# First projection of a hybrid attention layer: another order for VectorE, with two of its operations one K-tile further ahead

## The chip, the core and the metric

The kernel runs on one core of a Trainium2 chip. The core has a matrix engine (TensorE, PE in the profile; its weight loads are listed apart as PEld), VectorE (DVE), ScalarE (ACT), GpSimd (POOL), and SyncE (SP), which here issues all transfers. Each engine works through its own list of instructions in order and waits at semaphores for the others. The metric is the time of one execution on the device in microseconds (us); lower is better.

## The reference

One decoder layer for 512 rows of 1024 values, in float32. A vector `c` gives a shift, a scale and a gate for each of the 1024 columns; the normalised input is scaled and shifted, and one large matrix `w_in` gives all queries, keys, values and gates of two groups of heads.

```python
mod = jax.nn.silu(c) @ w_ada + b_ada
shift, scale, gate = jnp.split(mod, 3, axis=-1)
h = rms_norm(x, norm_gain) * (1 + scale[:, None, :]) + shift[:, None, :]
proj = h @ w_in
...
o_a = banded_gqa(qa, ka, heads(v_a, A_KV), SWA_WINDOW, rel_bias[:, :A_HEADS], sinks)
...
o_cmp, o_sel = nsa_cmp_sel(qb, k_cmp, v_cmp, k_sel, heads(vs, B_KV), bias_b)
o_win = banded_gqa(qb, k_win, heads(vw, B_KV), NSA_WINDOW, bias_b, None)
...
return x + gate[:, None, :] * out
```

## The kernel before

**Splitting numbers.** Products are made with operands of reduced precision, each split in a high part and a low part, and summed as high times high, high times low, low times high. For weights the high part is a copy on ScalarE (line 269 in the first projection, line 175 later), and the low part a subtraction on VectorE (lines 272 and 176). For the input `h` the high part `hh` and a full copy `hf` are made on ScalarE (line 283), and the low part `hl` = `hf` - `hh` on VectorE (line 286).

**First projection.** It makes the 768 columns of queries, keys and values of head group A, for all 512 rows at once, in six banks of accumulators. The 1024 inner values are worked through in eight K-tiles of 128, numbered 0 to 7. For each, `first_proj(k, n)` issues three passes of eight matmuls: pass 0 is `hh` with the weights' high part, pass 1 `hh` with the weights' low part, pass 2 `hl` with the weights' high part (lines 293 and 294). A tile needs, ahead of these passes:

- its weights (`load_wst`, one transfer, a ring of four), `weights_high(k)` on ScalarE and `weights_low(k)` on VectorE. The tiles `swh` and `swl` are asked for with three buffers each;
- its input, transposed, times the rows' norm: `scaled(k, ...)` on VectorE (line 277), in place in `xTp`;
- its modulation, two columns of `AB`. For tiles 0 and 1 TensorE computes them (`mod_pe`, `mod_col`), and `mod_ab` puts them in place (lines 238 and 239). For tiles 2 to 7 VectorE does, in `mod_rows(k)`: two row sums over 1024 values of `w_ada` each (line 243, one for the shift and one for the scale, each followed by a short read-out of the accumulator) and a small product (line 249). The rows of `w_ada` come through a ring of four (`load_ada`);
- `h_high(k)` on ScalarE (line 283: `hh` in two halves, then `hf`), which reads the scaled input and `AB`, and `h_low(k)` on VectorE.

**What sets the order.** This part is written inside `in_order(tc)` (line 300), which ties each instruction to the one traced before it on the same engine. So what the code says there, from top to bottom, is each engine's order, SP's transfers included. In the loop of line 410, the loads for tile k + 4 come first, then passes 0 and 1 of tile k, then `new_tile(k + 1)`, then pass 2 of tile k. At k = 3 the table `rest` and the first weights of the later projections are queued on SP as well (`load_next`, line 156: two halves of `kv_cmp`, two of `kv_sel`, one of `kv_win_g`). At k = 7, `split_to("kv_cmp", 3, 0)` splits the weights `kv_cmp` in four pieces, taken in turn from the first and the second half (`raws[g, p % 2]`).

In `new_tile(k)` VectorE has the order: weights' low part of tile k, the two row sums and the product of tile k + 1, input's low part of tile k, scaling of tile k + 1. ScalarE has: `hh` and `hf` of tile k, weights' high part of tile k + 1.

**Behind it.** After the block come the squares of the queries and keys (line 444 and on), their norms (`prep_a`, with the row sums of line 568), the keys' scaling (line 549) and transposition on TensorE (line 554), and the attention of group A. Meanwhile TensorE is fed by further projections: `kv_cmp` (line 491, 48 matmuls), `kv_sel` and `kv_win_g` (line 481), and so on. There the order on each engine isn't written out by hand: a planner makes it from its own costs and due times, and assigns the memory, where tiles whose use doesn't overlap by its plan can share a place.

Of the kernel before, what the change touches and what calls it, by code (L numbers as in the profile page):

```python
# [34 lines left out]
PE_MOD = (0, 1)  # L35
# [47 lines left out]
def hybrid_layer_kernel(ctx, tc, A, out):  # L83
# [30 lines left out]
    cT, prm, ident = first[:, 0:8], first[:, 8:40], first[:, 40:168]  # L114
# [85 lines left out]
    ada, wst = {}, {}  # L200
# [14 lines left out]
    AB = con.tile([128, 8, 2], F32, name="AB")  # L215
# [19 lines left out]
    def mod_ab(k):  # L235

        pc = pcs.pop(k)
        DVE.tensor_tensor(AB[:, k, 1:2], pc[:, 0:1], prm[:, k:k + 1], op=OP.add)
        DVE.scalar_tensor_tensor(AB[:, k, 0:1], pc[:, 1:2], prm1[:, k:k + 1], prm[:, 24 + k:25 + k],
                                 op0=OP.add, op1=OP.mult)  # L240

    def row_sum(w, init, out):
        DVE.tensor_tensor_reduce(out=w, in0=w, in1=scb, scale=1.0, scalar=init, op0=OP.mult, op1=OP.add, accum_out=out)

    def mod_rows(k):

        row_sum(ada[k][:, 0], prm[:, k:k + 1], AB[:, k, 1:2])
        row_sum(ada[k][:, 1], prm1[:, k:k + 1], modt[:, k:k + 1])
        DVE.tensor_tensor(AB[:, k, 0:1], modt[:, k:k + 1], prm[:, 24 + k:25 + k], op=OP.mult)

# [15 lines left out]
    def weights_high(k):  # L266

        ws[k] = (stp.tile([128, 768], F32R, name="swh", bufs=3), stp.tile([128, 768], F32R, name="swl", bufs=3))
        ACT.activation(ws[k][0], wst[k], AF.Copy)

    def weights_low(k):
        DVE.tensor_tensor(ws[k][1], wst[k], ws[k][0].bitcast(F32), op=OP.subtract)

    def scaled(k, by, parts=(slice(0, S),)):
        y[k] = xT[k]
        for c in parts:
            DVE.tensor_tensor(y[k][:, c], xT[k][:, c], by[:, c], op=OP.mult)

    def h_high(k, parts=(slice(0, S),)):
        hf[k] = T2(F32, "hf")  # L280
        for t in (hh[k], hf[k]):
            for c in (parts if t is hh[k] else parts[:0] + (slice(0, S),)):
                ACT.activation(t[:, c], y[k][:, c], AF.Identity, bias=AB[:, k, 1:2], scale=AB[:, k, 0:1])

    def h_low(k):
        DVE.tensor_tensor(hl[k], hf[k], hh[k].bitcast(F32), op=OP.subtract)
# [13 lines left out]
    with in_order(tc) as begun:  # L300
# [85 lines left out]
        rb = stp.tile([128, S], F32, name="rb")  # L386
# [6 lines left out]
        scaled(1, rbp)  # L393
        h_low(0)
        weights_high(1)

        def new_tile(k):

            if k in PE_MOD:
                mod_ab(k)  # L400
            h_high(k, halves)
            weights_low(k)
            if k < 7:
                weights_high(k + 1)
                if k + 1 not in PE_MOD:
                    mod_rows(k + 1)
            h_low(k)
            if k < 7:
                scaled(k + 1, rb)
        for k in range(8):  # L410
            if k + NR < 8:
                load_ada(k + NR)
                load_wst(k + NR)
            if k == LW - 1:
                SP.dma_start(rest[:, 0:960], A["rest"])
                for _ in range(5):
                    load_next()
            first_proj(k, 0)
            if k + 1 in PE_MOD:
                for _ in mod_pe(k + 1):  # L420
                    pass
            first_proj(k, 1)
            if k + 1 in PE_MOD:
                mod_col(k + 1)
            if k < 7:
                new_tile(k + 1)
            first_proj(k, 2)
            if k == 7:
                split_to("kv_cmp", 3, 0)
# [683 lines left out]
```

## Time and profile before

| | |
|---|---|
| median of three runs | 315.12 us (314.93 to 315.32) |
| the profiled execution | 313.99 us |
| its span, first to last instruction | 312.0 us |
| granted TensorE clock | 1.00 throughout |
| first matmul of the first projection (line 293) | 15.01 us |
| first matmul behind it (line 491) | 53.28 us |

The page's chain of work that ended last, by engine and by line of the kernel:

```profile
PE 82%; DVE 11%; ACT 3%; DMA 2%; issue 1%; SPq 0%; DVEq 0%; ACTq 0%
PE pj L491 30%; PE s L885 8%; PE sq L293 8%; PE po L960 8%; PE pj L481 7%; PE pt L943 4%; PE pt L933 4%; PE skv L294 4%; PE s L610 3%; DMA xf<-in_xn 2%; DVE wl L176 2%; DVE qs L541 2%; PE po L966 1%; DVE pa L890 1%; DVE qn L529 1%
```

How to read the views. A row of the timeline has the start, the duration, the engine, the line of the kernel, the operation, the tiles written and read, the shapes and the count; in brackets stands idle time of the engine just ahead of it and what ended it. Consecutive starts are closer together than the durations say, since the end of one operation overlaps the start of the next; the distance from start to start is what an operation costs its engine. A row of the waits has who waited and for whom, the total in us, the times, and the longest. "Released by" is inferred by the profiler from semaphores. The first projection is some 12% of the span: lines 293 and 294 are 8% and 4% of the chain.

### The profile page before, as it was taken

To read this page: it belongs to the slowest core of one execution; us is meant where nothing else is said; L and a number is where in the kernel's file an instruction comes from. 1 tells how busy PE (TensorE), PEld (TensorE's weight loads), DVE (VectorE), ACT (ScalarE), POOL (GpSimd) and SP (SyncE) were. 2 spreads that over 40 slices of the span, in tenths; PEclk is the share of its full clock that TensorE was granted. 3 is DMA by queue.
4 is the path that set the end of the run, shared out by engine and by line. 5 is a ranking of instruction groups with operands and counts; after the bars stand their busy time and mean duration, and the time that the engine had idled before them with its cause. 6 is when DMAs were issued, how large, how long until landed. Compare 5 with 4: busy or idle time off the path is not lost.

```text
span 312.0 us, 5882 instructions
## 1 busy us (share of the span) xinstructions
PE 303.3 (97%) x2131; PEld 252.5 (81%) x2131; DVE 238.0 (76%) x665; ACT 196.5 (63%) x473; POOL 3.8 (1%) x21
## 2 busy tenths in 40 slices
PE   8899999999999999999999999999999999999995
PEld 4577788789988889989878688779788878788885
DVE  4769998999886467786999999986977887455221
ACT  5765468777967675967867657696667776413000
POOL 1000000000000000000000000000000000000000
PEclk9999999999999999999999999999999999999999
DMA  7998947890184734041341252304530150024401
GB/s 285 381 395 292 413 151 261 278 292 23 32 273 138 220 115 139 3 134 36 106 166 68 67 168 68 105 1 137 158 114 0 51 154 2 0 69 135 134 34 69
DMA packets 27420, 44.21 MB, mean 142 GB/s; under 512 B 1712, under 2 KB 19408, under 8 KB 27392
## 3 DMA queue, kind: packets, MB, share of 16 engines
q1 hardware_dynamic: 27392, 43.84, 41.7%
q8 instruction: 17, 0.28, 0.4%
q14 instruction: 11, 0.09, 0.1%
HBM read 41.70 MB, written 2.14 MB: 141 GB/s over the span
## 4 chain that ended last, share of the span: by engine, by line
PE 82%; DVE 11%; ACT 3%; DMA 2%; issue 1%; SPq 0%; DVEq 0%; ACTq 0%
PE pj L491 30%; PE s L885 8%; PE sq L293 8%; PE po L960 8%; PE pj L481 7%; PE pt L943 4%; PE pt L933 4%; PE skv L294 4%; PE s L610 3%; DMA xf<-in_xn 2%; DVE wl L176 2%; DVE qs L541 2%; PE po L966 1%; DVE pa L890 1%; DVE qn L529 1%
## 5 line engine op out<-in xcount | busy, mean ns | idle before, releaser
L176 DVE TENSOR_TENSOR wl<-raw,wh 128x512 fp32r<-128x512 f32 (+1 forms) x52 | 35.5, 692 | 17.1 <-PE pj L491 10.8
L175 ACT ACTIVATE wh<-raw 128x512 fp32r<-128x512 f32 (+1 forms) x52 | 31.4, 634 | 26.0 <-PE pj L491 25.0
L481 PE MATMUL pj<-wh,hh 128*128 128x256 f32 (+1 forms) x128 | 36.7, 287 | 0.0
L481 PE MATMUL pj<-wl,hh 128*128 128x256 f32 (+1 forms) x128 | 36.5, 285 | 0.0
L481 PE MATMUL pj<-wh,hl 128*128 128x256 f32 (+1 forms) x128 | 36.3, 284 | 0.0
L897 ACT ACTIVATE pp<-pp,nm 128x256 f32<-128x256 f32 (+2 forms) x48 | 29.2, 610 | 10.8 <-DVE nm L890 10.5
L491 PE MATMUL pj<-hh,wh 128*128 128x512 f32 x80 | 32.5, 406 | 0.0
L491 PE MATMUL pj<-hl,wh 128*128 128x512 f32 x80 | 31.7, 397 | 0.0
L491 PE MATMUL pj<-hh,wl 128*128 128x512 f32 x80 | 31.7, 396 | 0.0
L890 DVE CUSTOM_DVE_ANT_0 pp<-s,bias 128x256 f32<-128x256 f32 (+2 forms) x48 | 25.3, 551 | 2.7 <-PE s L885 2.6
L491 PE MATMUL pj<-yh,wl 128*128 128x512 f32 (+1 forms) x72 | 26.6, 372 | 0.0
L491 PE MATMUL pj<-yl,wh 128*128 128x512 f32 (+1 forms) x72 | 26.4, 369 | 0.0
L491 PE MATMUL pj<-yh,wh 128*128 128x512 f32 (+1 forms) x72 | 26.2, 369 | 0.0
L481 PEld LDWEIGHTS pj<-wh,hh 128*128 128x128 f32 x128 | 24.1, 188 | 0.4 <-issue 0.3
L481 PEld LDWEIGHTS pj<-wh,hl 128*128 128x128 f32 x128 | 24.2, 189 | 0.0
L481 PEld LDWEIGHTS pj<-wl,hh 128*128 128x128 f32 x128 | 24.1, 188 | 0.0
L885 PE MATMUL s<-kTb,qs 128*128 128x256 f32 (+2 forms) x96 | 23.0, 357 | 0.0
L918 DVE TENSOR_SCALAR pp<-pp,rr,grev 128x256 f32<-128x256 f32 (+2 forms) x48 | 21.1, 475 | 0.5
L491 PEld LDWEIGHTS pj<-hh,wh 128*128 128x128 f32 x80 | 15.1, 189 | 4.0 <-issue 1.5
L897 ACT ACTIVATE pa<-pa,nm 128x257 f32<-128x257 f32 (+1 forms) x32 | 15.3, 480 | 4.3 <-DVE nm L890 2.4
L944 ACT COPY ptT<-pt 128x384 f32<-128x384 f32 (+1 forms) x32 | 15.6, 529 | 3.8 <-PE pt L943 3.2
L934 ACT COPY ptT<-pt 128x512 f32<-128x512 f32 (+1 forms) x28 | 15.3, 550 | 4.3 <-PE pt L933 3.8
(244 smaller groups left out, 695.6 us busy)
## 6 DMA issues: line engine op xcount, KB each, us to landing
ada_ring<-in_w_ada_ss SPq DMA_DIRECT2D x16, 512.0 KB, 8.7
raw<-in_w_cmp SPq DMA_DIRECT2D x8, 512.0 KB, 4.6
raw<-in_w_gate SPq DMA_DIRECT2D x8, 512.0 KB, 5.0
raw<-in_w_o SPq DMA_DIRECT2D x8, 512.0 KB, 4.6
wst_ring<-in_w_qkv_a SPq DMA_DIRECT2D x8, 384.0 KB, 10.1
xr<-in_xT SPq DMA_DIRECT2D x8, 256.0 KB, 2.8
bias<-line_d SPq DMA_DIRECT2D x8, 256.0 KB, 3.3
raw<-in_w_q_b SPq DMA_DIRECT2D x4, 512.0 KB, 4.8
```

Source lines behind the costliest of these rows:

```text
L175: ACT.activation(wh, src, AF.Copy)
L176: DVE.tensor_tensor(wl, src, wh.bitcast(F32), op=OP.subtract)
L293: PE.matmul(pj_q[tb], lt, w[:, 0:512], start=f, stop=l, skip_group_check=True)
L481: PE.matmul(bank[:, t * n:(t + 1) * n], h[:, tb * 128:(tb + 1) * 128], w[:, k % 2, :], start=k == 0 and m == 0, stop=k == 7 and m == 2)
L491: PE.matmul(bank, w, h[:, cols], start=k == 0 and m == 0, stop=k == 7 and m == 2)
L885: PE.matmul(ps, qs[h][:, 128 * i:128 * i + 128], k[:, hl_, lo:lo + n], start=hl_ == 0, stop=hl_ == 1)
L890: DVE.tensor_tensor_reduce(out=P[:, g, 0:w], in0=ps[:, 0:w], in1=bt, scale=1.0, scalar=init, op0=OP.add, op1=OP.min, accum_out=nm[:, g:g + 1])
L897: ACT.activation(P[:, g, 0:e], P[:, g, 0:e], AF.Exp, bias=nm[:, g:g + 1], scale=-1.0, accum_out=dn[:, g:g + 1])
L918: DVE.tensor_scalar(v, v, rr[:, g:g + 1], gates[:, g, br:br + 1], op0=OP.mult, op1=OP.mult)
L934: ACT.copy(T[:, :, 0:nb, :], rev(pt[:, 0:2 * nb * 128].rearrange("p (g b q) -> p g b q", g=2, b=nb)))
L944: ACT.copy(T[:, 0:nb, :], rev(pt[:, 0:nb * 128].rearrange("p (b q) -> p b q", b=nb)))
L960: PE.matmul(o[64 * g:64 * g + 64, 128 * i:128 * i + 128], vb[:, 64 * g:64 * g + 64], sl["T"][g][:, b, :], start=first_of and b == 0, stop= ...
```

## The change

`mod_rows` is cut in two: `mod_shift` is the first row sum, `mod_scale` the second with the product. Ahead of the loop, `weights_low(1)` and `scaled(2, rb)` are issued. In `new_tile(k)` VectorE then has, for tiles 2 to 6: the first row sum of tile k + 1, the input's low part of tile k, the second row sum and the product of tile k + 1, the weights' low part of tile k + 1, the scaling of tile k + 2. For tile 1 the input's low part comes behind `mod_scale`; for tile 7 only the input's parts are left. ScalarE's, TensorE's and SP's orders in the block stay as they are, and so do the instructions and their sizes.

```diff
--- before.py
+++ after.py
@@ -242,9 +242,10 @@
     def row_sum(w, init, out):
         DVE.tensor_tensor_reduce(out=w, in0=w, in1=scb, scale=1.0, scalar=init, op0=OP.mult, op1=OP.add, accum_out=out)
 
-    def mod_rows(k):
-
+    def mod_shift(k):
         row_sum(ada[k][:, 0], prm[:, k:k + 1], AB[:, k, 1:2])
+
+    def mod_scale(k):
         row_sum(ada[k][:, 1], prm1[:, k:k + 1], modt[:, k:k + 1])
         DVE.tensor_tensor(AB[:, k, 0:1], modt[:, k:k + 1], prm[:, 24 + k:25 + k], op=OP.mult)
 
@@ -393,20 +394,28 @@
         scaled(1, rbp)
         h_low(0)
         weights_high(1)
+        weights_low(1)
+        scaled(2, rb)
 
         def new_tile(k):
 
             if k in PE_MOD:
                 mod_ab(k)
             h_high(k, halves)
-            weights_low(k)
-            if k < 7:
-                weights_high(k + 1)
-                if k + 1 not in PE_MOD:
-                    mod_rows(k + 1)
-            h_low(k)
-            if k < 7:
-                scaled(k + 1, rb)
+            if k == 7:
+                h_low(k)
+                return
+            weights_high(k + 1)
+            mod_shift(k + 1)
+            if k > 1:
+                h_low(k)
+            mod_scale(k + 1)
+            if k == 1:
+                h_low(k)
+            weights_low(k + 1)
+            if k < 6:
+                scaled(k + 2, rb)
+
         for k in range(8):
             if k + NR < 8:
                 load_ada(k + NR)
```

## The prediction

> **What bounds the kernel now.** The first page says TensorE. Then come the busy times of single stretches: two K-tiles of the first projection, then the time behind it.
>
> ```profile
> span 312.0 us, 5882 instructions
> PE 303.3 (97%) x2131; PEld 252.5 (81%) x2131; DVE 238.0 (76%) x665; ACT 196.5 (63%) x473; POOL 3.8 (1%) x21
> ...
> 28.92:33.60 4.68, 4.43 (x25) 3.67 (x25) 4.65 (x9) 2.54 (x4) 0.00 (x0) 1.00 1.00 385
> ...
> 42.95:47.63 4.68, 4.44 (x25) 3.68 (x25) 4.64 (x9) 2.54 (x4) 0.00 (x0) 1.00 0.03 9
> ...
> 53.28:62.10 8.82, 8.82 (x40) 6.95 (x38) 8.58 (x29) 6.74 (x17) 0.43 (x3) 1.00 0.89 296
> 62.10:75.00 12.90, 12.63 (x91) 11.31 (x91) 12.40 (x26) 8.97 (x21) 0.00 (x0) 1.00 0.62 198
> 75.00:90.00 15.00, 14.57 (x115) 13.78 (x114) 13.85 (x45) 13.11 (x37) 0.75 (x4) 1.00 0.29 90
> 90.00:110.00 20.00, 20.00 (x170) 17.23 (x170) 11.81 (x44) 12.89 (x39) 0.75 (x4) 1.00 0.64 207
> ```
>
> Columns: stretch, length, then busy time of PE, weight loads, VectorE, ScalarE, GpSimd, then the granted clock (1.00), the DMA share and GB/s. In both tiles VectorE works 4.64 or 4.65 of 4.68 us and TensorE 4.43; the tile at 42.95 takes as long with idle DMA engines (0.03) as the one at 28.92 with full ones (1.00). So VectorE sets the pace of this stage. Behind it both engines are nearly full up to 90, and from 90 on VectorE has room (11.81 of 20) while TensorE has none.
>
> Next the waits of the stage, and VectorE in order of time around its one hole and at the last tiles.
>
> ```profile
> ACT hh L283 <- DVE xTp L277: 12.8, 6, 2.1
> ...
> DVE AB L238 <- PE pj L233: 2.1, 1, 2.1
> ...
> PE sq L293 <- DVE hl L286: 1.4, 6, 0.2
> ```
> ```profile
> 17.06 0.69 DVE L286 TENSOR_TENSOR hl<-hf,hh 128x512 fp32r<-128x512 f32 x1
> 19.82 0.16 DVE L238 TENSOR_TENSOR AB<-pj,first 128x1 f32<-128x1 f32 x1 [2.07 <-PE pj L233]
> ...
> 20.02 0.95 DVE L272 TENSOR_TENSOR swl<-wst_ring,swh 128x768 fp32r<-128x768 f32 x1
> 20.88 1.28 DVE L243 CUSTOM_DVE_ANT_0 ada_ring<-ada_ring,scb,first 128x1024 f32<-128x1024 f32 x1
> ...
> 43.41 0.95 DVE L272 TENSOR_TENSOR swl<-wst_ring,swh 128x768 fp32r<-128x768 f32 x1
> 44.27 1.28 DVE L243 CUSTOM_DVE_ANT_0 ada_ring<-ada_ring,scb,first 128x1024 f32<-128x1024 f32 x1
> ...
> 45.48 1.28 DVE L243 CUSTOM_DVE_ANT_0 ada_ring<-ada_ring,scb,prm 128x1024 f32<-128x1024 f32 x1
> 46.69 0.08 DVE L243 DVE_READ_ACCUMULATOR2_ANT modt<- 128x1 f32 x1
> 46.80 0.16 DVE L249 TENSOR_TENSOR AB<-modt,first 128x1 f32<-128x1 f32 x1
> 46.88 0.69 DVE L286 TENSOR_TENSOR hl<-hf,hh 128x512 fp32r<-128x512 f32 x1
> 47.48 0.68 DVE L277 TENSOR_TENSOR xTp<-xTp,rb 128x512 f32<-128x512 f32 x1
> 48.08 0.95 DVE L272 TENSOR_TENSOR swl<-wst_ring,swh 128x768 fp32r<-128x768 f32 x1
> 50.04 0.69 DVE L286 TENSOR_TENSOR hl<-hf,hh 128x512 fp32r<-128x512 f32 x1 [1.00 <-ACT hf L283]
> ```
>
> From start to start a tile costs VectorE 0.86 (weights' low part, 43.41 to 44.27), 1.21 (first row sum), 1.40 (second with L249, 45.48 to 46.88), 0.60 (input's low part), 0.60 (scaling): 4.67, the whole period. Its only idle time between the first and the last tile is the 2.07 ahead of 19.82, waiting for tile 1's modulation from TensorE. ScalarE waits for the scaling (L277) six times, up to 2.1 us each, though the modulation is ready earlier: in tile 7 at 46.96 (46.80 + 0.16), with ScalarE's first work on it at 48.20. TensorE then waits at each low part (L286).
>
> ```profile
> 47.62 0.50 PE L293 MATMUL sq<-swh,hl 128*128 128x512 f32 x1 [0.24 <-DVE hl L286]
> ...
> 49.12 0.39 PE L293 MATMUL sq<-swh,hh 128*128 128x512 f32 x1
> ...
> 53.28 0.40 PE L491 MATMUL pj<-hh,wh 128*128 128x512 f32 x1
> ```
> ```profile
> 16.93 0.83 ACT L269 ACTIVATE swh<-wst_ring 128x768 fp32r<-128x768 f32 x1
> ...
> 48.20 1.10 ACT L283 ACTIVATE hh<-xTp,AB 128x256 fp32r<-128x256 f32 x2 [2.14 <-DVE xTp L277]
> 49.20 0.80 ACT L283 ACTIVATE hf<-xTp,AB 128x512 f32<-128x512 f32 x1
> ```
>
> Tile 6's last pass starts at 47.62, tile 7's three passes run from 49.12 to 53.28: 4.16 us, against the 4.68 that VectorE needs for a tile. The stage can't get faster in its middle; time is to be had at its two ends only.
>
> **The change part by part.**
>
> *Two operations go into the hole.* The weights' low part of tile 1 leaves its place behind the modulation (20.02), and the scaling of tile 2 its place behind tile 1's low part; both now come ahead of the wait. The weights' high part of tile 1 ends at 17.76 (16.93 + 0.83), so they run from about 17.85 to 19.31 (0.86 + 0.60), 0.5 us ahead of 19.82. That TensorE result isn't moved. The first row sum of tile 2 starts at 20.02 instead of 20.88.
>
> *Order in a tile.* Now: first row sum, input's low part, second row sum with L249, weights' low part of the next tile, scaling of the one after: the same five, 4.67 us. No instruction and no DMA is added or dropped. Tile 1 has its low part behind both sums. The modulation of tile 2 is ready at 20.02 + 1.21 + 1.40 = 22.63. Then 0.60 + 0.86 + 0.60 bring tile 3's first row sum to 24.69, with the low part behind it 1.21 + 0.60 + 1.40 to 27.90, and four more tiles of 4.68 to 46.62 for tile 7, where it stood at 46.88: **0.26 earlier**. Only so little, since each modulation now has the low part of the tile before ahead of it.
>
> *The end.* This is where it is paid back. Tile 7's input is scaled long before, so ScalarE starts on it as soon as the modulation is there. ScalarE's lag behind VectorE is 0.12 (48.20 against 48.08, the scaling's end by the next start), half of the 1.10 another 0.6: TensorE can start tile 7 at about 47.4 instead of 49.12. Tile 6 isn't in the way: it started one period earlier, at 42.7, and its 4.16 end at 46.9. Its low part is written from 44.6 to 45.3, ahead of its pass at 45.5. TensorE keeps waiting about 0.5 per tile, now for the high part. Sum of the stage: 47.4 + 4.16 = 51.55 against 53.28, **1.7 us earlier**: 1.46 for the hole and about 0.25 for the shorter way from the last modulation.
>
> *What is moved past.* The low part of tile k now stands behind the first row sum of tile k+1. It needs `hf`, which ScalarE has 1.9 after the modulation (0.12, then 1.00 from `hh` to `hf` and 0.80 for `hf`); VectorE gets there after 0.86 + 0.60 + 1.21 = 2.67. So no wait, 0.75 of cover. An accumulator's read-out stands ahead of it now, as ahead of L249, where the next start is 0.11 behind the read-out's (46.69 to 46.80). Whether the low part pays this no row of the stage shows; ahead of the other row sum it costs nothing (45.48 is both the next sum's start and 1.21 behind 44.27). I take nothing, since the low part doesn't need the value that is read; five tiles bound it at 0.55.
>
> *SP's queue.* Its loads wait for the row sums' and low parts' buffers; those come free a little earlier. One load matters: the second half of `kv_cmp`.
>
> ```profile
> SPq L156 <- DVE AB L249: 11.8, 1, 11.8
> ...
> SPq L156 <- ACT hf L283: 1.3, 1, 1.3
> ```
> ```profile
> 46.80 0.54 SPq L156 DMA_DIRECT2D raw<-in_w_kv_cmp x1
> ```
> ```profile
> 49.91 0.62 ACT L175 ACTIVATE wh<-raw 128x512 fp32r<-128x512 f32 x1
> ...
> 50.67 0.63 ACT L175 ACTIVATE wh<-raw 128x512 fp32r<-128x512 f32 x1
> ```
>
> The tile `raw` has no user on VectorE before, so what it waited 11.8 us for is memory that the row sums held. It is issued when the last sum is done, and ScalarE's second split of `kv_cmp` begins 3.87 later (50.67), 0.14 behind the end of the first (49.91 + 0.62): it waited for the load. With the change the last sum is done 0.26 earlier, so this split and all that VectorE does behind it move by **0.25, not by 1.7**.
>
> *What survives.* Behind the stage TensorE has 1.7 us in hand and VectorE 0.25. They meet at the first keys:
>
> ```profile
> 61.37 0.68 DVE L549 TENSOR_TENSOR kn<-kn,rest 128x512 f32<-128x512 f32 x1
> ```
> ```profile
> 62.11 0.65 PE L554 MATMUL pt<-first,kn 128*128 128x128 f32 x4
> ...
> 62.96 0.48 PE L491 MATMUL pj<-hh,wl 128*128 128x512 f32 x1
> ```
>
> `kn` is done at 62.05 and TensorE turns it at 62.11. If the order on TensorE stays, it comes to L554 at 60.4, waits until 61.85, and 0.25 is left. But behind the block that order is made by the planner, not by hand; there is work that doesn't need `kn` (the last ten of `kv_cmp`'s 48 matmuls stand behind L554, from 62.96 on, then `kv_sel`). Filling the gap keeps 1.7, as long as VectorE's part up to 90 follows: it was idle 0.24 + 0.50 + 1.15 = 1.9 in the three stretches from 53.28 to 90, which a better order may use. Between 0.25 and 1.7 I take **1.0**, the middle.
>
> A rule speaks against even this. The Trainium skill, page "Perfetto Trace Analysis", section "Identifying Performance Opportunities", says that improving a kernel generally means improving its most-contended engine; it takes occupancy as the measure for VectorE, and for TensorE the busy share of the weight loads, not of the matmuls. By that measure VectorE is the most contended engine up to 75, with 8.58 of 8.82 and 12.40 of 12.90 against 6.95 and 11.31 of weight loads. The trace agrees so far that VectorE sets the period of the stage; by the rule only its 0.25 would count behind it as well, and that is the first rival.
>
> **The rivals.**
>
> *VectorE decides behind the stage.* TensorE runs dry where it needs `kn`, and again where it needs the next columns from VectorE. For it: VectorE's 8.58 of 8.82 up to 62.1. Against it: independent work is there, and VectorE's 1.9 of idle time. 315.12 - 0.25 = 314.9.
>
> *All is kept.* From 90 on VectorE has 8 us of room in 20, TensorE none; if VectorE's postponed work fits there, 1.7 come through: 313.4.
>
> *Slower: the load of `kv_cmp`'s second half comes later.* Place: the split at 50.67, which had no slack. If the weights' low part of tile 1 can't go into the hole, because its buffer is in truth that of tile 0 (the code asks for three, but the load's wait shows memory being shared), it waits for tile 0's second pass:
>
> ```profile
> 19.16 0.28 PE L294 MATMUL skv<-swl,hh 128*128 128x256 f32 x1
> ```
>
> It starts at 19.5, the modulation of tile 2 comes 1.15 later than worked out, the last sum 0.9 later than before, the load and VectorE's chain behind it 0.9 later too, while TensorE, 0.55 early, waits at L554: **316.0**. It decides from the point where the first row sum of tile 2 starts after 20.28 (20.02 + 0.26). Memory of tiles held longer has the same end. Then the change also doesn't do what it says. For it only the sharing; against it the three buffers.
>
> **How the numbers follow.** The profiled execution took 313.99 us, 1.99 beside its span of 312.0. The median of the three runs is 315.12 (314.93 to 315.32), 1.13 above it; the gain is subtracted from the median. Forecast: 315.12 - 1.0 = **314.1**, chance 0.48, its own range 0.6 to 1.6 of gain (313.5 to 314.5). VectorE decides: 0.22. All kept: 0.12. Slower: 0.14. Another order behind that costs or gives by chance: 0.04. The range goes from 313.2 (all kept, with 0.2 for the measurement) to 315.5 (0.55 for the read-outs takes the 0.25 away and 0.3 more, with 0.1); it leaves out most of the slower case. 0.2% is 0.63 us, about what a measurement of this kernel can tell from no change. Faster by more: nine tenths of the forecast, all kept and a little of the rest, 0.58. Slower by more: 0.15. Within: 0.27.
>
> **What would show it.** Right: VectorE's hole ahead of L238 under 0.6; tile 2's first row sum at 20.0; L283 waits for AB, not for `xTp`; TensorE's waits in L293 go from `hl` to `hh`; the first L491 near 51.6; the load of `kv_cmp` near 46.55 and the second split near 50.4. Wrong: a period other than 4.68; the first L491 later than 52.5; the split later than 50.67. Whether 1.0 is right shows at L554 and by 90: how far L554 stands behind the first L491, and how much TensorE is idle between them.

## The result and the profile after

| | before | after |
|---|---|---|
| median, same chip, four runs each | 315.22 us (314.93 to 315.32) | 313.60 us (313.25 to 313.81) |
| ratio, 95% interval | | 0.9949 (0.9933 to 0.9965): 1.1 to 2.1 us less |
| the profiled execution, its span | 313.99, 312.0 us | 313.25, 311.4 us |

The changed kernel is faster by 1.6 us; 314.1 was forecast. In it, line 250 is the old 249, 270 the old 269, 273 the old 272, 278 the old 277, 284 the old 283, 287 the old 286, 294 the old 293; behind the block 9 is added (500 for 491, 558 for 549, 563 for 554).

**Where to count from.** TensorE's timeline of the changed kernel: the first matmul of the first projection, that of tile 7, the first of `kv_cmp`, and the step to the first keys:

```profile
15.73 0.50 PE L294 MATMUL sq<-swh,hh 128*128 128x512 f32 x1 [0.59 <-ACT hh L390]
...
48.60 0.50 PE L294 MATMUL sq<-swh,hh 128*128 128x512 f32 x1 [0.28 <-ACT hh L284]
...
52.87 0.40 PE L500 MATMUL pj<-hh,wh 128*128 128x512 f32 x1
...
62.92 0.39 PE L500 MATMUL pj<-hl,wh 128*128 128x512 f32 x1
63.15 0.60 PE L563 MATMUL pt<-first,kn 128*128 128x128 f32 x4
```

The stage begins at 15.73 where it began at 15.01, though nothing of the change stands ahead of it. Both kernels were therefore profiled once more, and each stage is counted from its own first matmul:

| execution | first matmul | first of `kv_cmp` | stage | span | first matmul to the span's end |
|---|---|---|---|---|---|
| before | 15.01 | 53.28 | 38.27 | 312.0 | 297.0 |
| before, again | 15.36 | 53.65 | 38.29 | 312.4 | 297.0 |
| after | 15.73 | 52.87 | 37.14 | 311.4 | 295.7 |
| after, again | 14.96 | 52.10 | 37.14 | 310.6 | 295.6 |

The start wanders by 0.8 us from execution to execution; what comes behind it repeats within 0.1 in these two pairs. On this scale the change takes 1.13 from the stage and 1.3 to 1.4 from the end, inside the interval of the times. From the stage's end to the span's end it is 258.7 before and 258.5 after: behind the stage nothing of the gain is lost. Below, "stage" means the third of these columns and "end" the last. Of every other kernel below, one execution was profiled.

**VectorE** in the changed kernel, around the former hole, at tile 3 and at the last modulation (timeline):

```profile
18.51 0.96 DVE L273 TENSOR_TENSOR swl<-wst_ring,swh 128x768 fp32r<-128x768 f32 x1
19.39 0.69 DVE L278 TENSOR_TENSOR xTp<-xTp,rb 128x512 f32<-128x512 f32 x1
20.54 0.16 DVE L238 TENSOR_TENSOR AB<-pj,first 128x1 f32<-128x1 f32 x1 [0.47 <-PE pj L233]
20.62 0.21 DVE L239 SCALAR_TENSOR_TENSOR AB<-pj,prm,first 128x1 f32<-128x1 f32 x1
20.74 1.27 DVE L243 CUSTOM_DVE_ANT_0 ada_ring<-ada_ring,scb,first 128x1024 f32<-128x1024 f32 x1
...
26.63 0.08 DVE L243 DVE_READ_ACCUMULATOR2_ANT AB<- 128x1 f32 x1
26.63 0.68 DVE L287 TENSOR_TENSOR hl<-hf,hh 128x512 fp32r<-128x512 f32 x1
...
28.55 0.16 DVE L250 TENSOR_TENSOR AB<-modt,first 128x1 f32<-128x1 f32 x1
29.05 0.96 DVE L273 TENSOR_TENSOR swl<-wst_ring,swh 128x768 fp32r<-128x768 f32 x1 [0.34 <-issue]
...
47.75 0.16 DVE L250 TENSOR_TENSOR AB<-modt,first 128x1 f32<-128x1 f32 x1
47.83 0.96 DVE L273 TENSOR_TENSOR swl<-wst_ring,swh 128x768 fp32r<-128x768 f32 x1
49.78 0.69 DVE L287 TENSOR_TENSOR hl<-hf,hh 128x512 fp32r<-128x512 f32 x1 [0.99 <-ACT hf L284]
```

The two operations stand in the hole, of which 0.47 is left; tile 2's first row sum is at 20.74, that is 20.02 and the late start of 0.72. New is the row at 29.05: everywhere else L273 follows L250 after 0.08 (47.75 to 47.83), here after 0.50. "issue" means that the profile shows nothing that VectorE waited for.

The waits of the stage, and ScalarE and SP at its end:

```profile
ACT hh L284 <- DVE AB L250: 10.7, 5, 2.6
...
PE sq L294 <- ACT hh L284: 0.7, 3, 0.3
```
```profile
47.94 1.09 ACT L284 ACTIVATE hh<-xTp,AB 128x256 fp32r<-128x256 f32 x2 [2.18 <-DVE AB L250]
...
49.65 1.66 ACT L175 ACTIVATE wh<-raw 128x512 fp32r<-128x512 f32 x3
```
```profile
34.74 4.80 SPq L156 DMA_DIRECT2D raw<-in_w_kv_cmp  x2
```

ScalarE now waits for the modulation, no longer for the scaling. The second half of `kv_cmp` was issued at 39.0 (34.74 + 4.80, less the 0.54 that one issue took before); before, it was issued at 46.80. Its wait shows that the planner has given its tile other memory: before, it waited 11.8 for the product behind the last row sum, now 2.9 for one of TensorE's passes (`SPq L156 <- PE skv L295`). So the second split no longer waits for a load, and three splits run in one from 49.65.

Busy times of stretches, two of which were shown of before (53.28:62.10 and 62.10:75.00):

```profile
43.72:48.40 4.68, 4.44 (x24) 3.66 (x24) 4.65 (x9) 2.50 (x5) 0.00 (x0) 1.00 0.10 33
...
53.28:62.10 8.82, 8.82 (x39) 7.07 (x39) 8.28 (x27) 6.88 (x16) 0.43 (x3) 1.00 0.89 290
62.10:75.00 12.90, 12.45 (x93) 11.35 (x91) 12.13 (x26) 8.60 (x19) 0.00 (x0) 1.00 0.65 191
```

In the stage a tile is as long as before (4.68, VectorE 4.65): the gain is at the ends. Behind it TensorE is full up to 62.10 although it came earlier.

### The profile page after: what moved, and what is told of

The parts are those of the page before. It is cut to its first block, busy times and chain, and to the rows that moved or that the text cites. A ratio compares the mean times of both kernels' runs of the same rounds, so it can differ in the third digit from the quotient of the medians.

```text
span 311.4 us, 5871 instructions
## 1 busy us (share of the span) xinstructions
PE 303.4 (97%) x2131; PEld 253.0 (81%) x2131; DVE 238.1 (76%) x665; ACT 196.4 (63%) x473; POOL 3.8 (1%) x21
## 4 chain that ended last, share of the span: by engine, by line
PE 72%; DVE 19%; ACT 3%; DMA 2%; issue 2%; SPq 0%; DVEq 0%; ACTq 0%
PE pj L500 30%; PE po L969 8%; PE s L894 8%; PE pj L490 7%; DVE ada_ring L243 5%; PE pt L952 4%; PE pt L942 4%; PE s L619 3%; DMA xf<-in_xn 2%; PE sq L294 2%; DVE swl L273 2%; DVE wl L176 1%; PE po L975 1%; DVE hl L287 1%; DVE pa L899 1%
## 5 line engine op out<-in xcount | busy, mean ns | idle before, releaser
L500 PE MATMUL pj<-hh,wh 128*128 128x512 f32 x80 | 32.5, 406 | 0.0
L500 PE MATMUL pj<-hh,wl 128*128 128x512 f32 x80 | 31.7, 397 | 0.0
L500 PE MATMUL pj<-hl,wh 128*128 128x512 f32 x80 | 31.6, 395 | 0.0
L500 PE MATMUL pj<-yh,wl 128*128 128x512 f32 (+1 forms) x72 | 26.6, 371 | 0.0
L500 PE MATMUL pj<-yl,wh 128*128 128x512 f32 (+1 forms) x72 | 26.4, 369 | 0.0
L500 PE MATMUL pj<-yh,wh 128*128 128x512 f32 (+1 forms) x72 | 26.2, 369 | 0.0
L500 PEld LDWEIGHTS pj<-hh,wh 128*128 128x128 f32 x80 | 15.1, 188 | 3.9 <-issue 1.3
L500 PEld LDWEIGHTS pj<-hh,wl 128*128 128x128 f32 x80 | 15.0, 188 | 3.4
```

The lines of the kernel that those rows point to most:

```text
L500: PE.matmul(bank, w, h[:, cols], start=k == 0 and m == 0, stop=k == 7 and m == 2)
```

## The experiments

The theory (T): the filled hole and the shorter way at the end shorten the stage, and TensorE keeps this behind it, since the planner gives it other work. Rivals: what counts behind the stage is VectorE's chain, which the earlier load moved (R1); the filled hole alone makes the gain (R2); the planner's order changed by chance (R3). All results, each beside the kernel before on the same chip (medians 314.25 to 314.43):

| kernel | median us | ratio (95%) | stage | end |
|---|---|---|---|---|
| after again | 312.67 | 0.9944 (0.9931 to 0.9956) | 37.14 | 295.6 |
| run ahead alone | 313.53 | 0.9969 (0.9957 to 0.9981) | 37.44 | 296.5 |
| low part between the sums alone | 314.15 | 0.9993 (0.9984 to 1.0003) | 38.14 | 297.1 |
| after, load late | 312.51 | 0.9946 (0.9934 to 0.9958) | 36.71 | 295.1 |
| run ahead alone, tile of its own | 313.55 | 0.9975 (0.9966 to 0.9984) | 37.42 | 296.2 |
| after, tile of its own | 312.77 | 0.9952 (0.9939 to 0.9965) | 37.12 | 295.7 |
| run ahead alone, load early | 313.45 | 0.9964 (0.9951 to 0.9977) | 37.43 | 295.9 |
| after, three empty operations | 312.65 | 0.9941 (0.9929 to 0.9953) | 36.73 | 295.3 |
| after, scaling on GpSimd | 314.82 | 1.0017 (1.0007 to 1.0027) | 38.73 | 297.4 |
| after, load late, tile 4's modulation on TensorE | 314.27 | 0.9995 (0.9987 to 1.0004) | 37.56 | 296.9 |

Some expectations take the stage to `kv_cmp`'s first weight load, 0.1 ahead of its first matmul: 37.0 there is 37.1 here.

### Both kernels again

> The changed kernel once more, beside the experiments. Theory T (VectorE's hole and the shorter way from the last modulation shorten the first projection, and TensorE keeps all of it behind): ratio 0.993 to 0.997 as before, that is 1.0 to 2.0 us less. From the first matmul of the first projection to the first matmul of kv_cmp's columns 37.1 us again, against 38.3 in the profile of the kernel before, wherever the projection itself starts. The start 0.72 us later and the late low part of tile 3's weights (0.34 of issue ahead of it) were seen in one execution: if they belong to the change, they are here again; if they are chance, the start is within 0.3 of 15.0 and the stage 36.7.

> The kernel before once more, for its profile: whether the start of the first projection varies from execution to execution. If it does, its first matmul lies anywhere from 15.0 to 15.8 and the full clock is granted anywhere from 4.5 to 6.3 us; the stage from its first matmul to the first of kv_cmp's columns is 38.3 within 0.1 either way.

Measured: the two rows of each kernel in the table of the section on the result. The start belongs to the execution, the late weights' low part of tile 3 to the kernel: in its second execution the same operation again stood 0.50 behind L250, with 0.34 of issue.

### The two halves of the change

The run ahead alone, as a diff against after:

```diff
             mod_shift(k + 1)
-            if k > 1:
-                h_low(k)
             mod_scale(k + 1)
-            if k == 1:
-                h_low(k)
+            h_low(k)
             weights_low(k + 1)
```

> One half of the change: the weights' low parts and the scaling one tile ahead, but the input's low part behind both row sums. VectorE does the same five operations per tile, the last modulation is ready 0.6 us earlier than in the changed kernel (46.0 on the clock of the profile before), but the low part of tile 6 comes behind it and holds TensorE's last pass of tile 6 until 46.75; tile 7 starts near 48.15. By T the stage takes 37.3 to 37.8 us from its first matmul to the first of kv_cmp (0.5 to 1.0 less than before) and the time falls by as much: ratio 0.997 to 0.998, slower than the changed kernel by 0.3 to 0.6. By rival R2 (the filled hole alone makes the gain) as the changed kernel, 0.993 to 0.996. By rival R1 (the earlier landing of kv_cmp's second half makes the gain behind the stage) also as the changed kernel if the load lands ahead of the first split of kv_cmp, which it does if it is issued near 46.

The low part between the sums alone, against after:

```diff
-        weights_low(1)
-        scaled(2, rb)
...
             h_high(k, halves)
+            weights_low(k)
...
-            weights_low(k + 1)
-            if k < 6:
-                scaled(k + 2, rb)
+            scaled(k + 1, rb)
```

> The other half alone: the input's low part between the two row sums, the weights' low parts and the scaling at their old places. The hole of 2.07 us ahead of tile 1's modulation stays empty, and ScalarE's high part of each tile still waits for the scaling that stands behind the modulation. By T the stage takes 38.1 us (0.16 less than before) and the time is that of the kernel before within 0.3 us: ratio 0.999 to 1.001. By a rival (the place of the low part shortens TensorE's wait in each tile, and this makes the gain) 1.0 us less: 0.997. By R3 (the planner behind the stage finds another order by chance) any ratio from 0.997 to 1.003 with a stage within 0.2 of before.

The second half alone does nothing: stage 0.13 shorter, end as before. Yet behind its stage the planner made the same new order as in the changed kernel, with 44 of `kv_cmp`'s matmuls ahead of the keys (its rows between 53.59 and 63.84; 38 before): that order alone gains nothing, and R3 falls as the whole cause. The run ahead alone takes 0.83 from the stage, as T had it, and R2 falls: it is not the same as the whole change, with its 1.13. What it lacks is seen in its TensorE's timeline at tiles 6 and 7:

```profile
47.32 0.50 PE L294 MATMUL sq<-swh,hl 128*128 128x512 f32 x1 [0.25 <-DVE hl L287]
...
48.82 0.39 PE L294 MATMUL sq<-swh,hh 128*128 128x512 f32 x1
```

Tile 6's last pass waits for the low part behind both sums, and tile 7 stands behind that pass. Between the sums, the low part frees tile 7. Each half needs the other.

But of 0.83 only 0.5 reached the end, against T. TensorE and ScalarE behind the stage in this kernel:

```profile
61.36 0.39 PE L497 MATMUL pj<-hh,wh 128*128 128x512 f32 x1
61.59 0.40 PE L497 MATMUL pj<-hl,wh 128*128 128x512 f32 x1
62.06 0.66 PE L560 MATMUL pt<-first,kn 128*128 128x128 f32 x4
```
```profile
48.40 0.62 ACT L175 ACTIVATE wh<-raw 128x512 fp32r<-128x512 f32 x1
50.62 1.68 ACT L175 ACTIVATE wh<-raw 128x512 fp32r<-128x512 f32 x3 [1.61 <-DMA raw<-in_w_kv_cmp]
```

Matmuls of `kv_cmp` start every 0.23; the keys' L560 starts 0.47 behind the last, so TensorE stood still for 0.24. That is the meeting at the first keys of the prediction, with VectorE late: `kn` is 0.60 earlier than before (61.31 - 15.55 = 45.76 against 61.37 - 15.01 = 46.36), the stage 0.83. Here the second split waited 1.61 for the load that has to wait for the last row sum. In this order 38 of `kv_cmp`'s 48 matmuls stand ahead of L560, as before; in the changed kernel it is 44 (the timeline's rows between 52.87 and 63.15), with no gap (62.92 to 63.15).

### The load of `kv_cmp`'s second half

After, with the load tied behind the last row sum, and the loads queued behind it:

```diff
+    def late_load():
+        g, h = pending.pop(0)
+        t = rawp.tile([128, 4, GW], F32, name="raw")
+        DVE.memset(t[:, 0, 0:1], 0.0)
...
             mod_scale(k + 1)
+            if k == 6:
+                late_load()
+                for _ in range(3):
+                    load_next()
...
-                for _ in range(5):
-                    load_next()
+                load_next()
```

> The changed kernel, with the second half of kv_cmp (and the loads queued behind it) tied behind the last row sum: one element of its tile is set by VectorE there, right ahead of the load. In the changed kernel this load had been issued 9 us ahead of that, since its memory was other. All times from the first matmul of the first projection: the last row sum is done at 32.0, the split follows 3.9 behind the issue, near 36.0 (34.4 in the changed kernel, 35.7 before), and VectorE's chain behind it (the keys' second operation) comes 1.2 to 1.5 later than in the changed kernel. The stage is as long as in the changed kernel (37.0). Theory T (TensorE has other work and refills its order): the end comes at most 0.4 later than in the changed kernel, ratio to before 0.995 to 0.997. Rival R1 (what counts behind the stage is VectorE's chain, and the early load moved it): the end comes 1.0 to 1.4 later than in the changed kernel, ratio 0.999 to 1.001. For R1 speaks that the kernel with only the run ahead lost 0.3 of its 0.83 behind the stage.

Its ScalarE, TensorE at the keys, and VectorE's two operations on the keys:

```profile
48.69 0.62 ACT L183 ACTIVATE wh<-raw 128x512 fp32r<-128x512 f32 x1
50.77 1.68 ACT L183 ACTIVATE wh<-raw 128x512 fp32r<-128x512 f32 x3 [1.45 <-PE skv L303]
```
```profile
62.02 0.40 PE L511 MATMUL pj<-hl,wh 128*128 128x512 f32 x1
62.26 0.60 PE L574 MATMUL pt<-first,kn 128*128 128x128 f32 x4
```
```profile
60.25 0.69 DVE L567 TENSOR_TENSOR kn<-kraw,n_y 128x512 f32<-128x512 f32 x1
...
61.47 0.68 DVE L569 TENSOR_TENSOR kn<-kn,rest 128x512 f32<-128x512 f32 x1
```

The same two operations in the changed kernel:

```profile
59.96 0.69 DVE L556 TENSOR_TENSOR kn<-kraw,n_y 128x512 f32<-128x512 f32 x1
...
62.16 0.68 DVE L558 TENSOR_TENSOR kn<-kn,rest 128x512 f32<-128x512 f32 x1
```

The split is late as wished: 50.77 - 15.21 = 35.56 from the first matmul, against 34.44 (49.65 + 0.52 - 15.73; the three of the changed kernel start 0.52 apart). It costs nothing: again 44 matmuls stand ahead of the keys, there is no gap, and the end is even 0.6 earlier than in the changed kernel, 0.43 of it in the stage (36.71), where the stall at tile 3 is gone. So the early load is not what makes the gain, and this part of R1 falls.

VectorE was late only for a while. The keys' first operation is 0.81 later from the first matmul than in the changed kernel (45.04 against 44.23); the second, which TensorE waits for, is not (46.26 against 46.43), since the planner moved an operation on the queries out from between the two, and the weights' low part between them did not have to wait. The run therefore doesn't show what a late `kn` would cost in the order with 44; the last experiment below does. In the changed kernel itself VectorE is no earlier at this point than before (46.43 against 46.36). TensorE comes through without a gap since six matmuls more stand ahead of the keys: without them, by an estimate, it would have been there at 63.15 - 6 x 0.23 = 61.77, and `kn` is done only at 62.84 (62.16 + 0.68). There T is right.

The opposite: the run ahead alone, with a tile of its own for that half. The control has the same edit on after.

```diff
+    rawc = con.tile([128, 4, GW], F32, name="rawc")
...
-            t = rawp.tile([128, 4, GW], F32, name="raw")
+            t = rawc if (g, h) == ("kv_cmp", 1) else rawp.tile([128, 4, GW], F32, name="raw")
```

> The kernel with only the run ahead (input's low part behind both row sums), and a tile of its own for the second half of kv_cmp, so that its load waits for no row sum. In the kernel with the run ahead alone ScalarE waited 1.6 us for this load at the second split, the stage was 0.83 shorter than before and the end, from the first matmul of the first projection, 0.53 earlier. Here the second split stands right behind the first, near 33.4 from that matmul instead of 35.1. R1: the end is 0.8 to 1.0 earlier than before, all of the stage's gain; ratio 0.997. T: no difference that can be measured to the run ahead alone (0.5 earlier), since TensorE has other work there.

> The changed kernel with the same tile of its own for the second half of kv_cmp, as a control for the two kernels beside it: its load was early already, so R1 and T both expect the changed kernel's time within 0.3 us, ratio 0.993 to 0.997. If it differs by more, the placement of memory itself counts (R3).

The control does as after. The other edit did not do what it was meant to: the load still waited 12.6 for the product behind the last row sum and was issued at 46.46, as without the edit, so even the named tile shared its memory. Why the split came 0.28 earlier all the same (50.33 - 15.54 = 34.79, against 50.62 - 15.55 = 35.07) was not traced; the end came 0.3 earlier. To make the memory really its own, GpSimd sets one element of it at the start of the kernel:

```diff
+        POOL.memset(rawc[:, 0, 0:1], 0.0)
```

> The run ahead alone again (input's low part behind both row sums), with a tile for the second half of kv_cmp that is set by GpSimd at the start of the kernel, so that its memory is its own and its load waits for no row sum; in the try before, the tile got the memory of the row sums in spite of its name, and the load was issued at 46.5 as without it. Expected from the first matmul of the first projection: the load issued behind the loads of the stage, near 19 to 24 (it was 31), the second split right behind the first, near 33.4 (35.07 with the run ahead alone), the stage 37.3. By R1 (in this order, with 38 of kv_cmp's matmuls ahead of the keys, TensorE's progress behind the stage follows VectorE's chain, and that the split): the end is 0.8 earlier than before or better, all of the stage's 0.84, where the run ahead alone kept 0.53; ratio 0.9970 to 0.9975. By T (TensorE fills in anyway): 0.5. If the order behind is another one (44 matmuls ahead of the keys), the run doesn't tell them apart.

The load is at 35.68 (20.4 from the first matmul), the splits run in one, and TensorE goes into the keys without a gap:

```profile
48.07 0.62 ACT L176 ACTIVATE wh<-raw 128x512 fp32r<-128x512 f32 x1
48.59 0.62 ACT L176 ACTIVATE wh<-rawc 128x512 fp32r<-128x512 f32 x1
```
```profile
61.24 0.40 PE L499 MATMUL pj<-hl,wh 128*128 128x512 f32 x1
61.49 0.66 PE L562 MATMUL pt<-first,kn 128*128 128x128 f32 x4
```

Same stage (37.43), same 38 matmuls, end 1.1 earlier than before instead of 0.5. So in the order with 38 the traces speak for R1: with VectorE in time the gain comes through. It is not shown beyond that: each end is one execution, the medians of the times are only 0.08 us apart (313.45 and 313.53), and of the 0.6 between the ends the gap at the keys accounts for 0.24.

### The stall at tile 3

```diff
         scaled(2, rb)
+        DVE.memset(modt[:, 0:1], 0.0)
+        DVE.memset(modt[:, 1:2], 0.0)
+        DVE.memset(modt[:, 1:2], 0.0)
```

> The changed kernel with three one-column writes of VectorE behind the scaling of tile 2, in the hole of 0.47 us ahead of tile 1's modulation; they do nothing for the result. The late weights' low part of tile 3 (0.42 behind its turn, released by nothing that the profile shows) was in all three executions of the changed order, also with another placement of memory, and not in the kernel with the late load, where one wait instruction of VectorE ahead of it was missing. If the stall hangs on the place in VectorE's stream of instructions, moving it by two takes it away or elsewhere: the second row sum pair from tile 4 on comes 0.4 earlier, the stage is 36.6 instead of 37.0 and the end 0.4 earlier. If it belongs to what is moved (loads, memory, the order of the operations), the stage stays 37.0. The three writes themselves fit the hole: the first row sum of tile 2 stays at 5.02 from the first matmul, 0.1 later at most.

```profile
28.44 0.16 DVE L250 TENSOR_TENSOR AB<-modt,first 128x1 f32<-128x1 f32 x1
28.52 0.96 DVE L273 TENSOR_TENSOR swl<-wst_ring,swh 128x768 fp32r<-128x768 f32 x1
```

Three operations more, and the stage is 0.41 shorter (36.73), the end 0.4 earlier. The stall hangs on the place in VectorE's stream of instructions. Counted in the traces, waits included, the stalled operation is VectorE's 64th instruction in all executions with the stall (after twice, after with its own tile, and the kernel with tile 4 on TensorE), ahead of which stand only a wait and an operation of 0.16. In the other kernels another instruction is the 64th, mostly behind one of 0.9 us. What causes it was not shown.

### Two tries to go on

The scaling of tiles 3 to 7 on GpSimd (on the control):

```diff
-            DVE.tensor_tensor(y[k][:, c], xT[k][:, c], by[:, c], op=OP.mult)
+            (POOL if k > 2 else DVE).tensor_tensor(y[k][:, c], xT[k][:, c], by[:, c], op=OP.mult)
```

> The kernel of the control with the scaling of the tiles 3 to 7 on GpSimd, which has nothing else to do in this stage: the run ahead makes room for an engine that is slow. If VectorE sets the pace, its tile falls from 4.67 to 4.07 us, TensorE's three passes (4.16) become the bound, and the stage loses up to 5 x (4.51 - 4.16) = 1.75: 35.3 to 36.3 from its first matmul to kv_cmp's, ratio to before 0.989 to 0.992. If the loads of the modulation's weights set the pace at those tiles, or GpSimd's work holds up VectorE's, the stage is 36.5 or more and the ratio 0.993 or more.

GpSimd, and VectorE at the same time and behind:

```profile
16.59 8.89 POOL L279 TENSOR_TENSOR xTp<-xTp,rb 128x512 f32<-128x512 f32 x5 [15.21 <-ACT rb L392]
```
```profile
18.36 2.05 DVE L274 TENSOR_TENSOR swl<-wst_ring,swh 128x768 fp32r<-128x768 f32 x1
...
24.25 2.31 DVE L244 CUSTOM_DVE_ANT_0 ada_ring<-ada_ring,scb,prm 128x1024 f32<-128x1024 f32 x1
...
27.29 0.95 DVE L274 TENSOR_TENSOR swl<-wst_ring,swh 128x768 fp32r<-128x768 f32 x1
28.16 1.28 DVE L244 CUSTOM_DVE_ANT_0 ada_ring<-ada_ring,scb,first 128x1024 f32<-128x1024 f32 x1
...
32.25 1.28 DVE L244 CUSTOM_DVE_ANT_0 ada_ring<-ada_ring,scb,first 128x1024 f32<-128x1024 f32 x1
```

The tile does fall to 4.09 (28.16 to 32.25). But GpSimd takes 1.78 for each, all at once from 16.59, and while it runs VectorE's low part takes 2.05 instead of 0.95 and a row sum 2.31 instead of 1.28. The Trainium skill, page "SBUF — State Buffer", section "SBUF: two separate sides", says that VectorE and GpSimd share a pair of memory ports under an exclusive lock, so that a VectorE operation with two inputs in that memory and a GpSimd operation that reads it exclude each other. These rows agree, without showing the lock itself: 2.05 and 2.31 for operations that start while GpSimd works (up to 16.59 + 8.89 = 25.48), 0.95 and 1.28 behind it. The stage is 1.6 longer than in after.

Tile 4's modulation on TensorE (`PE_MOD = (0, 1, 4)`, and its row sums left out), on the kernel with the late load:

```diff
-PE_MOD = (0, 1)
+PE_MOD = (0, 1, 4)
...
-            mod_shift(k + 1)
+            if k + 1 not in PE_MOD:
+                mod_shift(k + 1)
...
-            mod_scale(k + 1)
+            if k + 1 not in PE_MOD:
+                mod_scale(k + 1)
```

> The kernel with the late load, and the modulation of tile 4 worked out by TensorE, as that of the tiles 0 and 1 is, instead of by VectorE's two row sums. VectorE loses 2.6 us of work in the middle of the stage, TensorE gets the ten small matmuls that take it about 1.2 for tile 1. If VectorE sets the pace (period 4.67 against TensorE's 4.16 per tile), the stage is 35.7 to 36.3 instead of 36.6, and the ratio to before 0.991 to 0.994. If TensorE's added work is not covered, or the modulation comes late because VectorE now waits for TensorE, 36.6 or more.

```profile
31.52 0.69 DVE L286 TENSOR_TENSOR xTp<-xTp,rb 128x512 f32<-128x512 f32 x1
34.03 0.16 DVE L246 TENSOR_TENSOR AB<-pj,first 128x1 f32<-128x1 f32 x1 [1.82 <-PE pj L241]
...
36.19 0.69 DVE L295 TENSOR_TENSOR hl<-hf,hh 128x512 fp32r<-128x512 f32 x1 [0.67 <-ACT hf L292]
```
```profile
63.69 0.66 PE L576 MATMUL pt<-first,kn 128*128 128x128 f32 x4 [0.68 <-DVE kn L571]
```

VectorE saves 2.6 and gives back 1.82 waiting for TensorE's modulation, with all its later work queued behind, and 0.67 for ScalarE; the stall at tile 3 (0.33) is back. That is 0.2 more than was saved, and a hole like that of tile 1 was made anew. The stage is 37.56, 0.85 longer than with the late load alone; the rest of it, TensorE's own added work included, was not taken apart.

The last row is the case that the late load left open. Here 44 matmuls stand ahead of the keys too, but `kn` comes 1.46 later than in the changed kernel (62.95 - 15.06 = 47.89 against 46.43), and TensorE stands still for 0.68 waiting for it. Of the 0.71 that the stage is shorter than before, 0.1 reaches the end. So the order with 44 gives cover, not freedom: in both orders TensorE goes on when its other work is done and `kn` is there, whichever comes last.

## Why the prediction was right, and where not

**Pace and hole: right.** 4.68 per tile, the hole at 0.47 (under 0.6 was said), tile 2's first row sum at the forecast place. The second buffer's wait, the point of the slower rival, didn't come: the low part of tile 1 ran at 18.51. The low part behind a read-out costs nothing (both at 26.63), as taken.

**The end of the stage: the mechanism right, the size off.** 1.7 was forecast, 1.13 measured. The first L491, now L500, was to come near 51.6 and not later than 52.5; it came at 52.87, or 52.15 without the late start. Tile 7 was to start at 47.4, with the late start 48.1; it starts at 48.60. Of the 0.57 missing, 0.42 is the stall at tile 3, which no row of before could show; with it gone the stage gains 1.54. Another 0.11 is in the three passes: 4.27 (48.60 to 52.87), not 4.16, since the first matmul now stands behind a wait (0.50 long, where that of before was 0.39).

**The load: wrong.** "So this split and all that VectorE does behind it move by 0.25" took it that the tile `raw` stays on the memory of the row sums. It got other memory, and the load came 8 us earlier. The 0.25 for VectorE was wrong for a second reason, which has nothing to do with the load: tile 7's low part waits for `hf`, and `hf` moves with the shorter way from the last modulation. That low part came 0.98 earlier (50.04 - 15.01 against 49.78 - 15.73), and with the run ahead alone, whose load is as late as before, 2.05 earlier (48.53 - 15.55). What the early load adds is seen against the late one: the keys' first operation 0.81 earlier, and nothing at the second.

**What survives: mis-sized.** "Between 0.25 and 1.7 I take 1.0": all of the 1.13 survived, with 0.2 more. The reason stood there, that work is there to fill TensorE's gap, and the planner put 44 of 48 matmuls ahead of the keys instead of 38. The time came out near the forecast partly by luck: a gain taken too large was multiplied by a share taken too small.

**The rivals.** That all is kept came closest. That VectorE decides was the first rival, for which the Trainium skill's page "Perfetto Trace Analysis", section "Identifying Performance Opportunities", was cited. The runs bear it out where `kn` is late: with 38 matmuls ahead of the keys the run ahead lost 0.3 of its 0.83, 0.24 of it as a gap at the keys, and with 44 the kernel with tile 4 on TensorE lost 0.6 of its 0.7, with a gap of 0.68 there. They don't bear it out for the change itself: VectorE was no earlier at the keys than before, and TensorE kept its 1.13 all the same.

**A better kernel?** With the late load or the three empty operations the end comes 0.6 and 0.4 earlier than in the changed kernel; 0.4 of each is the stall. By the times (0.9946 and 0.9941, against 0.9944 for the change) neither is shown to beat it.

## What to carry to other kernels

Where one engine sets the pace, look for its holes at the ends of the stage, and fill them with work that it does later anyway; the middle stays as it is. Whether the gain lasts behind the stage depends on how much independent work the next engine has ahead of the first thing that it must wait for, and on how late that thing is. A load that waits for memory moves when an edit changes how long tiles are held, so read anew what it waits for in the changed kernel instead of carrying it over.

## What the runs showed of the hardware that wasn't expected

- The first projection began anywhere from 14.90 to 15.73 us in thirteen profiled executions, at 14.96 and at 15.73 in two executions of the changed kernel; counted from there, two executions of one kernel agreed within 0.1 us up to the end of the span.
- VectorE's 64th instruction in the trace came 0.42 late in the four executions in which only a wait and an operation of 0.16 stood right ahead of it, and in none of the nine others; three operations without effect took the delay away.
- With GpSimd multiplying two tensors, VectorE's low part of 128x768 took 2.05 instead of 0.95 us.
